# A two-layer attention trunk on one core: a sign flip moved behind a norm on ScalarE, two weight splits moved behind gate products on VectorE

## The chip, the cores and the metric

The kernel runs on one core of a Trainium2 chip. The metric is device microseconds of one execution. Three runs of the kernel before gave 819.14, 820.42 and 816.18 us, median 819.14 us. The execution that was profiled took 817.46 us.

The engines are called by the names that the profile uses: PE is TensorE's matmul, PEld its weight load, DVE is VectorE, ACT is ScalarE, POOL is GpSimd, SP is the queue that issues most of the loads.

## The reference, cut to what matters

Two decoder layers over 256 tokens of width 2048, then a final RMSNorm, all in float32.

```python
def rmsnorm(x, g):
    y = x * lax.rsqrt(jnp.mean(x * x, axis=-1, keepdims=True) + RMS_EPS)
    return y * g
# layer 0: forgetting attention, 32 heads of 64; logits += c[t] - c[s]
# layer 1: sliding window of 128, 32 query heads, 4 key heads, learned sinks:
m = jnp.maximum(jnp.max(s, axis=-1, keepdims=True), sink)
e = jnp.exp(s - m)
denom = jnp.sum(e, axis=-1, keepdims=True) + jnp.exp(sink - m)
o = jnp.einsum('bnhgqk,bnkhd->bnqhgd', e / denom, vw)
# both layers
y = y * jax.nn.silu(gate)
x = x + y @ w_out
```

The sinks are one learned number per head; they take part in the maximum and in the denominator of the second layer's softmax. Each layer's input projection yields queries, keys, values and a gate.

## The kernel before, in words

**Weights.** Every weight matrix is streamed from HBM once, in pieces of 128 x 1024 floats (512 KB). A piece lands in one of four raw buffers (`wraw`, issued from SP). `load` then splits it into a rounded high part, a cast on ScalarE (L222), and the exact remainder, the low part, a subtraction on VectorE (L223); the two stand in one of five buffers `w`. A raw buffer is free again when its low part is made. TensorE multiplies the high part with the activations' high and low halves in one wide product (512 columns) and the low part with the activations' high half in a narrow one (256 columns). In most units two pieces go together: the wide products of the first, the wide products of the second, then the narrow products of the first and of the second. So a piece's high part is needed some microseconds before its low part.

**Units and groups.** A unit is 256 output columns: four pieces, accumulated over 16 tiles of the inner dimension into a PSUM tile `acc` (two of them). Each unit ends in a function that reads `acc`. In the second layer a group `SwaGroup` has a query unit (`q`: rotation at L839 to L889, then the split `stack_q`, L366 and L367) and a gate unit (`gate_consumer`, L324, L325, and `silu`, L312 to L319). A group has two pairs of heads. A pair's scores go to the PSUM tile of the tag `S`, of which there is one (`ps_s2`, L453 to L460); L462 and L389 on VectorE add the mask and take the extreme, L337 and L902 on ScalarE are the exponentials, L353 and L356 normalise, L475 on VectorE transposes into `turned`. For every two groups `values` multiplies the probabilities with the values. For groups 1, 3 and 5 two of the four blocks of this product lie in the tag `S` tile (`psy_s`) and two in `psy` tiles; `some` multiplies them with the gates (the gate products, L962 for the first two blocks, L966 for the others) and then splits the result for the output projection (`spread`, L518 and L519). The next scores `ps_s2` can only be written when L962 has read `psy_s`, because both use the one tile.

**Order.** TensorE's instructions stay in the order in which the program issues them. Work of the attention is put between the matmuls by a count of steps: `after(n, fn)` calls `fn` n steps later. On the other engines a list scheduler orders the instructions, by its own estimates and by priorities (`tc.high_priority`); each engine then executes its list in that order.

**The sinks.** They are loaded by a DMA on POOL's queue during the first layer (L633, from the bias of the pair with head 8). L741, written in the second layer's `norm` right after its 1/rms, multiplies them by -1 on ScalarE into `sinks[:, 1, :]`; the score reductions of the second layer (L389) read this copy. The scheduler is free to place L741.

Of the kernel before, what the change touches and what calls it, by code (L numbers as in the profile page):

```python
# [10 lines left out]
F32 = mybir.dt.float32  # L11
F32R = mybir.dt.float32r
AF = mybir.ActivationFunctionType
ALU = mybir.AluOpType
# [45 lines left out]
def trunk(  # L60
# [16 lines left out]
    nc = tc.nc  # L77


    def mm(*args, **kw):  # L80
        tc.keep_in_program_order(nc.tensor.matmul(*args, **kw))  # L81
# [25 lines left out]
    def after(steps, fn):  # L107
        due.setdefault(clock[0] + max(steps, 1), []).append(fn)
# [23 lines left out]
    def inv_rms(sums, name, ps):  # L132
        for i, a in enumerate(sums):
            mm(ps[:, 0:S], ones, a, start=i == 0, stop=i == len(sums) - 1)
        v = cpool.tile([P, S], F32, tag="rms_v", name=f"v_{name}")
        nc.vector.tensor_scalar(v, ps[:, 0:S], 1.0 / D, EPS, op0=ALU.mult, op1=ALU.add)
        both = cpool.tile([P, S + 2], F32, tag="rms_r", name=f"r_{name}", bufs=2)
        r = both[:, 0:S]
        nc.scalar.activation(r, v, AF.Ln)
        nc.scalar.activation(r, r, AF.Exp, scale=-0.5)  # L140

        t = cpool.tile([P, S], F32, tag="rms_t", name=f"t_{name}")
        nc.vector.scalar_tensor_tensor(out=t, in0=r, scalar=-0.5, in1=r, op0=ALU.mult, op1=ALU.mult)
        nc.vector.tensor_mul(t, t, v)
        nc.vector.scalar_tensor_tensor(out=r, in0=t, scalar=1.5, in1=r, op0=ALU.add, op1=ALU.mult)

        for th in range(2):
            nc.vector.tensor_tensor_reduce(
                out=t[:, 0:P], in0=r[:, th * P : (th + 1) * P], in1=ident, scale=1.0, scalar=0.0,
                op0=ALU.mult, op1=ALU.add, accum_out=both[:, S + th : S + th + 1],  # L150
            )
        return both

    def split_x(kt, layer):
        g = g_sb[:, layer, kt : kt + 1]
        nc.scalar.activation(xs[:, kt, 0, :], xT[:, kt, :], AF.Copy, scale=g)  # L156
        nc.vector.scalar_tensor_tensor(
            out=xs[:, kt, 1, :], in0=xT[:, kt, :], scalar=g, in1=xs[:, kt, 0, :].bitcast(F32),
            op0=ALU.mult, op1=ALU.subtract,
        )  # L160
# [25 lines left out]
    state = {}  # L186
    asked = set()

    def ask(unit, p, eng):
        src, off, total, _, _ = unit.parts[p]  # L190
        n = unit.n
        if off == 0 and (unit, p) not in asked:
            asked.add((unit, p))
            given = unit.stages[p] if p < len(unit.stages) else None
            if given is None:
                raw = wpool.tile([P, 1024], F32, tag="wraw", name="wraw", bufs=4)
            else:
                pool, tag, size, bufs = given
                raw = pool.tile([P, size], F32, tag=tag, name="wraw", bufs=bufs)
            raw = raw[:, 0 : total * n]  # L200
            if isinstance(src, tuple):

                raw = raw.rearrange("p (g k n) -> p g k n", g=2, k=total)
                for g in range(2):
                    eng.dma_start(out=raw[:, g], in_=src[g])
                raw = raw.rearrange("p g k n -> p k g n")
            else:
                raw = raw.rearrange("p (k n) -> p k n", n=n)
                eng.dma_start(out=raw, in_=src)
            unit.raw = raw  # L210

    def load(unit, p):
        src, off, _, _, s = unit.parts[p]
        n = unit.n
        ask(unit, p, nc.sync)
        raw = unit.raw[:, off : off + s, :]
        w = wpool.tile([P, 2048], F32R, tag="w", name="w")
        w = w[:, 0 : 2 * s * n].rearrange("p (k h n) -> p k h n", h=2, n=n)
        high, low = w[:, :, 0, :], w[:, :, 1, :]
        if isinstance(src, tuple):  # L220
            high, low = (a.rearrange("p k (g n) -> p k g n", g=2) for a in (high, low))
        state["split"] = nc.scalar.copy(high, raw)  # L222
        nc.vector.tensor_tensor(out=low, in0=raw, in1=high.bitcast(F32), op=ALU.subtract)  # L223
        loaded[unit, p] = w

    def block(unit, p, c):
        _, _, _, kt0, s = unit.parts[p]
# [77 lines left out]
    def whole(src, kind, consume, **kw):  # L305
        return Unit(quarters(src), kind, consume, **kw)
# [221 lines left out]
    ones_row, z, a = (once[0:H, i * S : (i + 1) * S] for i in range(3))  # L528
# [182 lines left out]
    def square_into(sums, m):  # L711
        s = work.tile([P, 2, S], F32, tag="half", name="sq", bufs=HALVES)[:, 0, :]
        nc.scalar.activation(s, xT[:, m, :], AF.Square)  # L713
        if m == 0:
            acc = cpool.tile([P, S], F32, tag="ssq", name="acc", bufs=2)
            sums.append(acc)
            nc.gpsimd.tensor_copy(acc, s)  # L717
        else:
            nc.gpsimd.tensor_add(sums[0], sums[0], s)  # L719
# [5 lines left out]
    def to_layer1(m):  # L725
        split_x(m, 1)
        square_into(sums1, m)
        if m == KT - 1:

            def norm():  # L730
                nonlocal swa
                fox_scope.__exit__(None, None, None)
                swa = ctx.enter_context(tc.tile_pool(name="swa", bufs=2))
                state["r1"] = r = inv_rms(
                    sums1, "n1", ps_s.tile([P, 2, 512], F32, tag="S", name="ps_n1")[:, 0, :]
                )
                rope = swa.tile([P, 2, S], F32, name="rope_c", bufs=1)
                nc.sync.dma_start(out=rope, in_=rope_d)
                nc.vector.tensor_mul(rope, rope, r[:, 0:S].unsqueeze(1).to_broadcast([P, 2, S]))
                state["rr"] = rope  # L740
                nc.scalar.mul(state["sinks"][:, 1, :], state["sink"], -1.0)  # L741
                after(20, tail_residual)

            after(19, norm)
# [135 lines left out]
    class SwaGroup(Group):  # L880
# [50 lines left out]
        def some(self, together, mine, pair=None):  # L931

            kv = self.u // 2
            turned, vr = self.other.pts, state["vr"]
            banks = {} if pair is None else {a: pair[:, a] for a in range(2)}
            for a in mine:
                if a not in banks:
                    banks[a] = ps_t.tile([P, 512], F32, tag="T", name="psy")
            wanted = {}
            for a in mine:  # L940
                by_block = [(0, list(range(a + 1))), (1, list(range(a, NB + a + 1)))]
                wanted[a] = [(qb, k, k == ks[0], k == ks[-1]) for qb, ks in by_block for k in ks]
            for i in range(max(map(len, wanted.values()))):
                for a in mine:
                    if i >= len(wanted[a]):
                        continue
                    qb, k, first, last = wanted[a][i]
                    rows = slice(a * B, (a + 1) * B)
                    for hh in range(2):
                        out = banks[a][hh * HD : (hh + 1) * HD, 0 : 8 * B]  # L950
                        out = out.rearrange("p (n b i) -> p n b i", n=4, b=2)[:, :, qb, :]
                        o = qb * P + k * B
                        mm(
                            out, vr[k][rows, kv * HD : (kv + 1) * HD], turned[rows, :, hh, o : o + B],
                            start=first, stop=last, skip_group_check=True, tile_position=(a * B, hh * HD),
                        )
            for g, G in enumerate(together):
                y = G.gt.rearrange("p j (b a i) -> p a (j b) i", b=2, a=NB)
                here = slice(g * 4 * B, (g + 1) * 4 * B)
                if pair is not None:  # L960
                    both = pair[:, :, here].rearrange("p a (m i) -> p a m i", i=B)
                    nc.vector.tensor_mul(y[:, 0:2], both, y[:, 0:2])  # L962
                for a in mine:
                    if pair is None or a >= 2:
                        one = banks[a][:, here].rearrange("p (m i) -> p m i", i=B)
                        nc.vector.tensor_mul(y[:, a], one, y[:, a])  # L966
                if NB - 1 in mine:
                    self.spread(G)

    swa_units = [whole(swa_in_d[8], "wgt", swa_k), whole(swa_in_d[9], "tok", swa_v)]  # L970
    swa_groups = [SwaGroup(u) for u in range(8)]
# [64 lines left out]
    def fetch(upto):  # L1036
        while fetched[0] < min(upto, len(stream)):
            load(*stream[fetched[0]])
            fetched[0] += 1
# [127 lines left out]
```

## Time and profile before

| | |
|---|---|
| three runs | 816.18, 819.14, 820.42 us |
| profiled execution | 817.46 us |
| its span, first to last instruction | 815.7 us |
| busy share: PE, PEld, DVE, ACT, POOL | 99%, 87%, 77%, 65%, 8% |
| DMA, mean over the span | 186 GB/s |
| mean granted clock of TensorE | 0.998 |
| chain that ended last, by engine | PE 84%, DVE 8%, ACT 3%, DMA 3%, issue 1% |

The span leaves out 1.76 us of the execution's own time. A row of the timeline reads: start in us, duration in us, engine, line, operation, what is written from what, shapes, count, and in brackets how long the engine stood idle before it and what ended that. A row of the waits reads: who waited for whom, total us, times, longest.

### The profile page before, as it was taken

What the parts mean: (1) busy time and instruction counts of PE and PEld (TensorE: products, weight loads), DVE (VectorE), ACT (ScalarE), POOL (GpSimd) and SP (SyncE); (2) the same over time, 40 slices, a digit from 0 to 9 for tenths busy, and PEclk for the clock granted to TensorE, in tenths of its full rate; (3) what the DMA queues carried; (4) which work ended last, traced back from release to release, by engine and by line L of the source; (5) the groups of instructions that cost most, each with busy time, mean ns of one, the idle gap of its engine ahead of it and who ended that gap; (6) DMA issues with size and microseconds to landing.
All of it is one profiled execution on the core that took longest, in us unless ns stands there. A gap on an engine that the chain in (4) does not pass through costs nothing.

```text
span 815.7 us, 13805 instructions
## 1 busy us (share of the span) xinstructions
PE 804.4 (99%) x5090; PEld 705.6 (87%) x5090; DVE 628.5 (77%) x1132; ACT 526.6 (65%) x979; POOL 65.5 (8%) x102
## 2 busy tenths in 40 slices
PE   9999999999999999999999999999999999999996
PEld 8988878888888888888888888888888888888886
DVE  6988765888568875788848667669989889896645
ACT  6775665665657665576747455567788777875552
POOL 1013020010000100000002110200000000001210
PEclk9999999999999999999999999999999999999999
DMA  9766556565664666565465655765545465465632
GB/s 292 256 205 230 187 178 200 181 205 170 200 190 153 213 198 191 169 211 186 156 187 173 196 183 197 201 181 184 173 136 185 151 205 171 134 210 170 204 130 104
DMA packets 47730, 151.84 MB, mean 186 GB/s; under 512 B 5696, under 2 KB 7648, under 8 KB 47664
## 3 DMA queue, kind: packets, MB, share of 16 engines
q1 hardware_dynamic: 44640, 141.84, 54.0%
q0 software_dynamic: 1872, 7.67, 3.4%
q10 hardware_dynamic: 1152, 1.47, 0.5%
q8 instruction: 40, 0.66, 0.3%
q14 instruction: 26, 0.21, 0.1%
HBM read 148.55 MB, written 2.41 MB: 185 GB/s over the span
## 4 chain that ended last, share of the span: by engine, by line
PE 84%; DVE 8%; ACT 3%; DMA 3%; issue 1%; DVEq 0%; SPq 0%; ACTq 0%
PE acc L81 78%; DVE w L223 3%; DMA wraw<-in_swa_in_dram 2%; PE ps_s L81 2%; PE psy L81 2%; PE pt L84 1%; ACT st L337 1%; DVE turned L475 1%; DVE st L389 1%; ACT st L356 1%; ACT w L222 0%; DMA wraw<-in_vf_dram 0%; DVE q L367 0%; DVE st L462 0%; ACT gate_e L312 0%
## 5 line engine op out<-in xcount | busy, mean ns | idle before, releaser
L81 PE MATMUL acc<-xs,w 128*128 128x512 f32 (+1 forms) x2624 | 474.8, 339 | 0.0
L81 PEld LDWEIGHTS acc<-xs,w 128*128 128x128 f32 x2624 | 404.7, 190 | 52.8 <-issue 0.7
L223 DVE TENSOR_TENSOR w<-wraw,w 128x1024 fp32r<-128x1024 f32 (+4 forms) x277 | 322.4, 1180 | 107.5 <-ACT w L222 106.7
L222 ACT CAST w<-wraw 128x1024 fp32r<-128x1024 f32 (+4 forms) x277 | 274.5, 1008 | 136.6 <-PE acc L81 89.8
L81 PE MATMUL acc<-ys,w 128*128 128x512 f32 (+1 forms) x960 | 169.4, 337 | 0.0
L81 PEld LDWEIGHTS acc<-ys,w 128*128 128x128 f32 x960 | 147.7, 189 | 20.4 <-issue 0.5
L81 PE MATMUL acc<-w,xs 128*128 128x512 f32 (+2 forms) x512 | 111.1, 364 | 0.5 <-ACT w L222 0.5
L81 PEld LDWEIGHTS acc<-w,xs 128*128 128x128 f32 x512 | 86.8, 191 | 14.3 <-ACT w L222 0.8
L337 ACT ACTIVATE st<-st,mx 128x128 f32<-128x128 f32 (+1 forms) x128 | 56.6, 444 | 12.7 <-DVE mx L640 11.6
L295 ACT COPY half<-acc 128x512 f32<-128x512 f32 x56 | 32.5, 581 | 9.1 <-PE acc L81 8.5
L81 PE MATMUL ps_s<-kk,q 128*128 128x256 f32 (+1 forms) x160 | 30.8, 306 | 0.2 <-DVE gt L962 0.2
L719 POOL TENSOR_TENSOR acc<-acc,sq 128x256 f32<-128x256 f32 x28 | 23.7, 848 | 89.0 <-ACT sq L713 87.9
L81 PEld LDWEIGHTS ps_s<-kk,q 128*128 128x128 f32 x160 | 24.6, 189 | 3.9 <-issue 1.2
L125 POOL TENSOR_SCALAR_AFFINE_SELECT bc<-bc 128x256 f32<-128x256 f32 x32 | 22.1, 708 | 71.4 <-DMA bc<-negc_d 71.4
L627 POOL DMA_DIRECT2D bc<-negc_d x16 | 8.9, 554 | 214.3 <-DVE st L420 152.3
L312 ACT ACTIVATE gate_e<-gt 128x512 f32<-128x512 f32 x16 | 10.1, 632 | 24.6 <-DVE gt L325 24.6
L429 ACT COPY pts<-pt 128x384 f32<-128x384 f32 x32 | 15.2, 476 | 14.9 <-PE pt L84 14.9
L475 DVE STREAM_TRANSPOSE turned<-st 128x768 f32<-128x768 f32 x16 | 15.6, 977 | 11.5 <-ACT st L356 11.5
L717 POOL COPY acc<-sq 128x256 f32<-128x256 f32 x2 | 1.3, 672 | 286.3 <-ACT sq L713 286.3
L337 ACT ACTIVATION_READ_ACCUMULATOR st<-st,mx 128x1 f32 x128 | 24.0, 188 | 0.0
L356 ACT ACTIVATE st<-st,rl 128x128 f32<-128x128 f32 x64 | 23.9, 445 | 0.0
L156 ACT ACTIVATE xs<-xT,g_sb 128x256 fp32r<-128x256 f32 x32 | 15.5, 501 | 12.8 <-DVE xT L699 12.0
(144 smaller groups left out, 591.1 us busy)
## 6 DMA issues: line engine op xcount, KB each, us to landing
wraw<-in_fox_in_dram SPq DMA_DIRECT2D x96, 512.0 KB, 4.5
wraw<-in_swa_in_dram SPq DMA_DIRECT2D x72, 512.0 KB, 4.4
wraw<-in_fox_out_dram SPq DMA_DIRECT2D x32, 512.0 KB, 4.0
wraw<-in_swa_out_dram SPq DMA_DIRECT2D x32, 512.0 KB, 4.3
wraw<-in_fox_in_dram SPq DMA_DIRECT2D x54, 256.0 KB, 4.4
bc<-negc_d POOLq DMA_DIRECT2D x16, 384.0 KB, 5.2
wraw<-in_vf_dram SPq DMA_DIRECT2D x4, 288.0 KB, 4.8
xT<-in_xt_dram SPq DMA_DIRECT2D x2, 512.0 KB, 7.8
```

What stands on the lines that cost most here:

```text
L81: tc.keep_in_program_order(nc.tensor.matmul(*args, **kw))
L125: return nc.gpsimd.affine_select(out=ap, in_=ap, compare_op=ALU.is_ge, fill=NEG, base=base, pattern=pattern, channel_multiplier=mult,)
L156: nc.scalar.activation(xs[:, kt, 0, :], xT[:, kt, :], AF.Copy, scale=g)
L222: state["split"] = nc.scalar.copy(high, raw)
L223: nc.vector.tensor_tensor(out=low, in0=raw, in1=high.bitcast(F32), op=ALU.subtract)
L295: nc.scalar.copy(s, ps[:, :, S : 2 * S])
L312: nc.scalar.activation(e, z, AF.Abs)
L337: nc.scalar.activation(st[:, hh, rng], st[:, hh, rng], AF.Exp, scale=sign, bias=nm[:, qb, hh : hh + 1], accum_out=l[:, qb, hh : hh + 1],)
L356: nc.scalar.mul(st[:, hh, rng], st[:, hh, rng], rl[:, qb, hh : hh + 1])
L429: nc.scalar.copy(group.new_pts(self.j, hh)[:, hh, self.j, :], pt[:, 0 : 3 * P])
L475: nc.vector.transpose(turned.rearrange("p h k -> p (h k)"), self.st.rearrange("p h k -> p (h k)"))
L719: nc.gpsimd.tensor_add(sums[0], sums[0], s)
```

## The change

Three edits. The multiplication by -1 of the sinks (L741, in the changed kernel L752) is told to keep its place in the program, which is behind the two activations that make 1/rms of the second layer. `load` remembers the last two low parts. And after the gate products of groups 1, 3 and 5, `ahead_of_lows` adds an ordering edge, without a semaphore, from the last gate product to each of these two: they come later on VectorE than the products.

```diff
@@ load
         state["split"] = nc.scalar.copy(high, raw)
-        nc.vector.tensor_tensor(out=low, in0=raw, in1=high.bitcast(F32), op=ALU.subtract)
+        state["lows"] = [*state.get("lows", [])[-1:], nc.vector.tensor_tensor(
+            out=low, in0=raw, in1=high.bitcast(F32), op=ALU.subtract
+        )]
         loaded[unit, p] = w
+
+    def ahead_of_lows(ins):
+
+        for low in state["lows"]:
+            tc.add_manual_dep(
+                low.ins, ins.ins.name,
+                mybir.DependencyInfo(mybir.DependencyClass.NoSync, mybir.DependencyReason.DATA),
+                reason="ahead_of_lows",
+            )
@@ norm, in to_layer1
                 state["rr"] = rope
-                nc.scalar.mul(state["sinks"][:, 1, :], state["sink"], -1.0)
+                tc.keep_in_program_order(nc.scalar.mul(state["sinks"][:, 1, :], state["sink"], -1.0))
                 after(20, tail_residual)
@@ SwaGroup.some
-                        nc.vector.tensor_mul(y[:, a], one, y[:, a])
+                        last = nc.vector.tensor_mul(y[:, a], one, y[:, a])
                 if NB - 1 in mine:
                     self.spread(G)
+            if pair is not None:
+                ahead_of_lows(last)
```

The instructions are the same ones. On PE, POOL and SP their order is the same too; on ACT and DVE it differs as follows. (Lines from 224 on stand 11 higher in the changed kernel, from the end of `some` on 13.)

On ACT in the first layer, where the changed sign stood: `pts` are copies of transposed probabilities, `vg` are values, `w` are casts of weights, `st` are exponentials. Before:

```order
L222 CAST w_1183<-wraw_1181 128x4x256
L429 COPY pts_1193<-pt_1189 128x384
L741 ACTIVATE sinks_302<-sinks_302 128x32
L429 COPY pts_1193<-pt_1211 128x384
L600 ACTIVATE vg_1220<-acc_953,r_n0_492 128x512 x2
L222 CAST w_1225<-wraw_1223 128x4x256
L222 CAST w_1265<-wraw_1263 128x4x256
L337 ACTIVATE st_1195,l_1242<-st_1195,mx_1196 128x128
```

The changed kernel has these rows there without the third one. It stands instead on ACT behind 1/rms of the second layer (`r_n1`), ahead of a cast:

```order
L139 ACTIVATE r_n1_4958<-v_n1_4956 128x256
L140 ACTIVATE r_n1_4958<-r_n1_4958 128x256
L752 ACTIVATE sinks_302<-sinks_302 128x32
L222 CAST w_4991<-wraw_4989 128x4x256
L306 COPY half_5004<-acc_4901 128x512
```

On DVE at the gate products of group 1 (groups 3 and 5 have the same rows with other numbers): `q2` is the split of a query unit, `w` low parts, `gt` the gate products, `ys` their split, `st` the scores. Before:

```order
L367 TENSOR_TENSOR q2_5738<-rot_t_5729,q2_5738 64x2x256 x2
L223 TENSOR_TENSOR w_5776<-wraw_5774,w_5776 128x4x256
L223 TENSOR_TENSOR w_5789<-wraw_5787,w_5789 128x4x256
L962 TENSOR_TENSOR gt_5317<-psy_s_5815,gt_5317 128x2x4x32
L962 TENSOR_TENSOR gt_5574<-psy_s_5815,gt_5574 128x2x4x32
L966 TENSOR_TENSOR gt_5317<-psy_5816,gt_5317 128x4x32
L966 TENSOR_TENSOR gt_5574<-psy_5816,gt_5574 128x4x32
L966 TENSOR_TENSOR gt_5317<-psy_5817,gt_5317 128x4x32
L966 TENSOR_TENSOR gt_5574<-psy_5817,gt_5574 128x4x32
L223 TENSOR_TENSOR w_5892<-wraw_5890,w_5892 128x4x256
L519 TENSOR_TENSOR ys_81<-gt_5317,ys_81 128x2x256
L519 TENSOR_TENSOR ys_81<-gt_5574,ys_81 128x2x256
```

Now:

```order
L378 TENSOR_TENSOR q2_5738<-rot_t_5729,q2_5738 64x2x256 x2
L973 TENSOR_TENSOR gt_5317<-psy_s_5815,gt_5317 128x2x4x32
L973 TENSOR_TENSOR gt_5574<-psy_s_5815,gt_5574 128x2x4x32
L977 TENSOR_TENSOR gt_5317<-psy_5816,gt_5317 128x4x32
L977 TENSOR_TENSOR gt_5574<-psy_5816,gt_5574 128x4x32
L977 TENSOR_TENSOR gt_5317<-psy_5817,gt_5317 128x4x32
L977 TENSOR_TENSOR gt_5574<-psy_5817,gt_5574 128x4x32
L223 TENSOR_TENSOR w_5776<-wraw_5774,w_5776 128x4x256
L223 TENSOR_TENSOR w_5789<-wraw_5787,w_5789 128x4x256
L530 TENSOR_TENSOR ys_81<-gt_5317,ys_81 128x2x256
L530 TENSOR_TENSOR ys_81<-gt_5574,ys_81 128x2x256
L473 TENSOR_TENSOR st_5929<-ps_s2_5931,smask_291 128x2x128
```

The two low parts went behind all six products, and the low part `w_5892` behind the first step of the scores. The scheduler then also orders what follows in another way, up to the next query unit's split. On DVE at that unit's rotation (`rot`), before:

```order
L319 TENSOR_TENSOR gt_5903<-gt_5903,gate_e_5908 128x512
L841 STREAM_SHUFFLE rot_6062<-rot_t_6058 128x512
L223 TENSOR_TENSOR w_6047<-wraw_6045,w_6047 128x4x256
L844 TENSOR_TENSOR rot_t_6058<-rot_t_6058,rope_c_4967 128x512
L845 TENSOR_TENSOR rot_6062<-rot_6062,rope_c_4967 128x512
L475 STREAM_TRANSPOSE turned_6080<-st_6002 128x768
L889 TENSOR_TENSOR rot_t_6058<-rot_t_6058,rot_6062 128x512
L223 TENSOR_TENSOR w_6074<-wraw_6072,w_6074 128x4x256
L367 TENSOR_TENSOR q2_6067<-rot_t_6058,q2_6067 64x2x256 x2
```

Now:

```order
L852 STREAM_SHUFFLE rot_6062<-rot_t_6058 128x512
L486 STREAM_TRANSPOSE turned_6080<-st_6002 128x768
L855 TENSOR_TENSOR rot_t_6058<-rot_t_6058,rope_c_4967 128x512
L856 TENSOR_TENSOR rot_6062<-rot_6062,rope_c_4967 128x512
L330 TENSOR_TENSOR gt_5903<-gt_5903,gate_e_5908 128x512
L900 TENSOR_TENSOR rot_t_6058<-rot_t_6058,rot_6062 128x512
L223 TENSOR_TENSOR w_6047<-wraw_6045,w_6047 128x4x256
L223 TENSOR_TENSOR w_6074<-wraw_6072,w_6074 128x4x256
L378 TENSOR_TENSOR q2_6067<-rot_t_6058,q2_6067 64x2x256 x2
```

The low part `w_6047` went behind the rotation. The low parts `w_5976` and `w_5989`, which stood behind the second pair's extremes (L389), now stand ahead of them, and on ACT their casts stand ahead of the first pair's normalising (L356, now L367) instead of behind it, while the gate's activations (L312 and on) stand behind it.

## The prediction

> **What bounds the kernel now.** First the shares of the page, then the waits of TensorE's two queues, since a change on ScalarE and VectorE can only bring what TensorE waits for them.
>
> ```profile
> span 815.7 us, 13805 instructions
> PE 804.4 (99%) x5090; PEld 705.6 (87%) x5090; DVE 628.5 (77%) x1132; ACT 526.6 (65%) x979; POOL 65.5 (8%) x102
> ...
> PE rows L81 <- DVE tail L800: 2.1, 1, 2.1
> PE pt L84 <- DVE st L348: 1.8, 1, 1.8
> ...
> PE ps_s L81 <- DVE gt L962: 0.2, 1, 0.2
> ...
> PEld pt L84 <- ACT st L337: 2.0, 1, 2.0
> ...
> PEld ps_s L81 <- issue: 1.2, 3, 0.6
> ```
>
> TensorE bounds it: 804.4 of 815.7 us are matmul. Besides the start and the tail there are two kinds of hole. One is a single wait of 1.8 us (matmul row) or 2.0 us (weight-load row) of transposes `pt` for normalised probabilities. The other is small and stands ahead of three score products `ps_s`: 0.2 us by the matmul row, 1.2 us in three by the weight-load row. The change is aimed at these two, so 2.0 to 3.2 us is all it can take away.
>
> **The sign of the sinks.** The timeline around the one big hole:
>
> ```profile
> 104.16 0.47 ACT L429 COPY pts<-pt 128x384 f32<-128x384 f32 x1
> ...
> 105.62 0.49 PE L84 MATMUL pt<-ident,st 128*128 128x128 f32 x3
> ...
> 105.87 1.17 PE L81 MATMUL acc<-w,xs 128*128 128x512 f32 x4
> ...
> 109.35 0.08 DVE L389 DVE_READ_ACCUMULATOR2_ANT mx<- 128x1 f32 x1
> ...
> 110.43 0.23 ACT L741 ACTIVATE sinks<-sinks 128x32 f32<-128x32 f32 x1 [5.80 <-DMA sinks<-in_sink_dram]
> ...
> 110.93 1.27 ACT L600 ACTIVATE vg<-acc,r_n 128x512 f32<-128x512 f32 x2
> 112.08 2.00 ACT L222 CAST w<-wraw 128x1024 fp32r<-128x1024 f32 x2
> ...
> 113.17 1.26 DVE L223 TENSOR_TENSOR w<-wraw,w 128x1024 fp32r<-128x1024 f32 x1 [3.73 <-ACT w L222]
> ...
> 114.94 0.41 ACT L337 ACTIVATE st<-st,mx 128x128 f32<-128x128 f32 x1 [0.86 <-DVE mx L640]
> ...
> 117.49 0.61 PE L84 MATMUL pt<-ident,st 128*128 128x128 f32 x3 [1.81 <-DVE st L348]
> ```
>
> ScalarE stands 5.80 us at the sign flip, until the sinks' DMA lands at 110.43. Queued behind it are a copy of `pts`, the values `vg`, two casts, and the exponentials of the next pair; VectorE's low part waits 3.73 us for the first of those casts, with the pair's extremes (L639, L640) behind it, and TensorE waits for the pair.
>
> Without the flip: the second `pts` copy can start when its transposes end (105.62 + 0.49 = 106.11) and takes 0.47, to 106.58. The values need the last `acc` products (105.87 + 1.17 = 107.04), so they run from 107.04 to 108.31. The casts follow without a wait in the old rows, to 110.31, the first one done at about 109.3. VectorE is free at 109.43, so its low part starts there instead of at 113.17. From its start to the exponentials took 114.94 - 113.17 = 1.77, which gives 111.20, and from there to the transposes on TensorE 117.49 - 114.94 = 2.55, which gives 113.75. TensorE itself only arrives at about 117.49 - 1.98 = 115.5. So the inputs are 1.75 us early, and the whole hole closes: **-2.0 us** (the weight-load row; -1.8 by the matmul row). If a cast had to wait for a landing or a buffer that the stall now hides, up to 1.75 us of that costs nothing.
>
> At its new place the flip has company:
>
> ```profile
> 501.18 0.42 ACT L140 ACTIVATE r_n<-r_n 128x256 f32<-128x256 f32 x1
> ...
> 502.41 1.05 ACT L222 CAST w<-wraw 128x1024 fp32r<-128x1024 f32 x1 [0.81 <-PE acc L81]
> ```
>
> Its 0.23 us fall into the 0.81 us in which the next cast waits for TensorE anyway, and its DMA landed some 390 us earlier: **0**. If that cover were gone, it would delay one cast by 0.23 us.
>
> **The two low parts.** The three places, seen on TensorE and VectorE (first and second place, and the third's weight load):
>
> ```profile
> 585.63 3.29 PE L81 MATMUL acc<-xs,w 128*128 128x256 f32 x18
> 585.66 2.36 DVE L223 TENSOR_TENSOR w<-wraw,w 128x1024 fp32r<-128x1024 f32 x2
> ...
> 587.94 0.75 DVE L962 TENSOR_TENSOR gt<-psy_s,gt 128x256 f32<-128x256 f32 x2
> 588.60 0.88 DVE L966 TENSOR_TENSOR gt<-psy,gt 128x128 f32<-128x128 f32 x4
> 588.80 0.77 PEld L81 LDWEIGHTS ps_s<-kk,q 128*128 128x128 f32 x6 [0.30 <-issue]
> 588.83 0.95 PE L81 MATMUL ps_s<-kk,q 128*128 128x256 f32 x6
> ...
> 635.68 3.29 PE L81 MATMUL acc<-xs,w 128*128 128x256 f32 x18
> ...
> 639.14 0.95 PE L81 MATMUL ps_s<-kk,q 128*128 128x256 f32 x6 [0.16 <-DVE gt L962]
> ...
> 689.25 0.77 PEld L81 LDWEIGHTS ps_s<-kk,q 128*128 128x128 f32 x6 [0.39 <-issue]
> ```
>
> The values' products have ended when `acc` resumes at 585.63, but the gate products only start at 587.94, behind 2.36 us of low parts. They free the one score tile at 588.69, and `ps_s` starts right then, at 588.83. With the products ahead they run from about 585.7 to 586.4 for the score tile, over 2 us before TensorE asks for it. These holes close too.
>
> Their size: the 18 matmuls ahead are 10 narrow and 8 wide. The pace of each comes from two pieces of the chain of waits, wide and then narrow:
>
> ```profile
> 88.17 2.32 PE acc L81 x10
> ...
> 164.51 1.18 PE acc L81 x10
> ```
>
> That is 0.232 and 0.118 us, so 18 need 10 x 0.118 + 8 x 0.232 = 3.04 us. They took 588.83 - 585.63 = 3.20 and 639.14 - 635.68 = 3.46: 0.16 and 0.42 lost; the third, whose weight-load gap of 0.39 lies between the first's 0.30 and the second's 1.2 - 0.30 - 0.39 = 0.5, about 0.25. Together 0.83, of which I leave some for the resumption after the values' products, which stays. Bounds 0.2 (matmul wait) and 1.2 (weight-load gaps); I take **-0.6 us**, nearer to the spacing of the matmuls than to either.
>
> [...]
>
> What the two low parts lose: `w_5776` ends some 1.5 us later (the six products, 587.94 to 589.48), near 588.4. Its narrow products come behind six scores, eight wide and eight narrow ones, 588.83 + 0.79 + 1.86 + 0.94 = 592.4. Free by 4 us; `w_5789` has more. **0**.
>
> **What moved further down.** The tightest is `w_6047`, now behind the rotation:
>
> ```profile
> 598.17 0.98 DVE L475 STREAM_TRANSPOSE turned<-st 128x768 f32<-128x768 f32 x1 [1.62 <-ACT st L356]
> ...
> 605.57 1.22 DVE L223 TENSOR_TENSOR w<-wraw,w 128x1024 fp32r<-128x1024 f32 x1
> 606.69 0.69 DVE L844 TENSOR_TENSOR rot_t<-rot_t,rope_c 128x512 f32<-128x512 f32 x1
> ...
> 609.36 1.23 DVE L223 TENSOR_TENSOR w<-wraw,w 128x1024 fp32r<-128x1024 f32 x1
> ...
> 612.65 0.88 PE L81 MATMUL ps_s<-kk,q 128*128 128x256 f32 x6
> ```
>
> The rows from 606.69 to 609.36 (2.67 us) go ahead of it, so it ends at 606.79 + 2.67 = 609.46 if VectorE keeps its pace. TensorE wants it ahead of eight narrow and eight wide matmuls that precede the scores at 612.65: 612.65 - 0.94 - 1.86 = 609.85, about 0.1 earlier once the first hole is gone. That leaves 0.3 us, where there were 3. What widens it: VectorE's wait of 1.62 us at 598.17 is now filled, as `w_5976` and `w_5989` stand there. I price it at **0**; between a gain of nothing and a loss of 1 us in each of three places (VectorE over a microsecond behind its old pace).
>
> **Sum.** -2.0 - 0.6 = -2.6 us. On the profiled execution: 817.46 - 2.6 = 814.9, of which 1.76 lie outside the span, which would be 813.1. The median shown lies 1.7 above that execution and would give 816.5. The four executions have a mean of 818.3, and I take that level: **815.7 us**.
>
> **The rivals.**
>
> *A: the new order waits for a landing (slower).* On ScalarE the casts of `w_5976` and `w_5989` now stand ahead of the first pair's normalising. The raw buffer of `w_5976` is the one that `w_5776` frees, so its load starts at 588.4 instead of 586.9.
>
> ```profile
> wraw<-in_swa_in_dram SPq DMA_DIRECT2D x72, 512.0 KB, 4.4
> ...
> 527.50 10.62 DMA wraw<-in_swa_in_dram
> ```
>
> With the usual 4.4 us it lands at 592.8; the cast's turn comes near 595, so nothing waits. With the 10.62 of the chain's longest it lands at 599.0, 4 us late; normalising, transposition and rotation, and with them `w_6047`, come 4 us late, of which the filled wait absorbs 1 at most: 3 us in each of three places, 9 - 2.6 = 6.4 slower, 824.7 us. It decides from landings over 7 us. For it: such a landing exists in this layer. Against: it stands where the values' own round trip loads the DMA. 5%.
>
> *B: VectorE runs short after all.* The 0.3 us at `w_6047` are overdrawn by 1 us a place: +3 - 2.6 = 0.4 slower, 818.7 us. For: VectorE shows next to no idle there but the 1.62. Against: just that wait is now filled. 9%.
>
> *C: the big hole is handed on.* The transposes wait for something that the flip hid (the landing of the casts' pieces), and only the small holes close: -0.6, 817.7 us. For: both casts ran in the shadow of the flip, so the rows don't show when their data came. Against: 1.75 us of margin. 8%.
>
> *D: the small holes don't close* (the scores wait for the query split instead): -2.0, 816.3 us. Against: that split is over when the low parts start at 585.66, 3 us ahead of the scores. 10%.
>
> The forecast has the remaining 68%.
>
> **How the numbers follow.** The three runs shown spread over 4.2 us, so two medians of three can differ by some 1.7 us by chance alone, and half a percent, 4.1 us, is about what can be told from no change. Faster by over 0.5% needs 1.5 us of such chance on top of -2.6, about one time in five: 0.68 x 0.2, with D's 0.1 x 0.12 and a little from the others, 0.16. Slower by over 0.5% is A and a sliver of B: 0.05. The rest, 0.79, is within. No case gains over 3.2 us by itself. The range for 8 in 10 goes from 812 (the bound of -3.2 and the chance spread downwards) to 819.5, which holds B, C and D; A is left out.
>
> **What would show it.** Right: ScalarE's wait of 5.80 us for the sinks' DMA is gone, the row of `pt` waiting for L348 near 115 us is gone, the gate products (now L973) start right behind the query split, and the three scores behind them show no weight-load gap; busy times of all engines stay as they are. Wrong: a wait of TensorE's narrow products for VectorE's low parts after each of the three places (B), a cast waiting for a landing ahead of L367 (A), or a new wait of `pt` for L222's followers (C). If the time fell by more than 4 us with only these holes closed, the reading of TensorE's idle time was too narrow.

## The result, and the profile after

The changed kernel took 814.67 us (median of 6 executions, 813.63 to 814.94), the kernel before, on the same chip, 818.80 us (median of 6, 816.18 to 820.42). The ratio is 0.995, with a 95% interval of 0.9933 to 0.9967: faster by half a percent, 4.1 us. The predicted time was 815.7 us. The range, 812 to 819.5 us, also holds the kernel before (818.80 us), so that the time fell in it says little of the mechanism; the change and the traces say more. The execution that was profiled took 814.94 us, where the sum had 814.9; but 4.1 us are more than the 2.6 us of that sum, and the times lie within 1.3 us of one another where those of the kernel before spread over 4.2 us. The experiments are about these two surprises.

First the page of the changed kernel: its span, the busy times by engine, and what TensorE's matmuls waited for.

```profile
span 813.2 us, 13799 instructions
PE 803.5 (99%) x5090; PEld 705.6 (87%) x5090; DVE 629.2 (77%) x1132; ACT 527.1 (65%) x979; POOL 62.5 (8%) x102
```

```profile
PE rows L81 <- DVE tail L811: 2.1, 1, 2.1
PE warm L81 <- DVE ones L118: 1.1, 1, 1.1
PE acc L81 <- ACT w L222: 0.8, 2, 0.5
```

The rows of `pt` and of `ps_s` are gone, and nothing new stands beside the tail and the start. The span is 2.5 us shorter; the busy times are within 1 us of what they were, but for POOL's, 3.0 us less. The timeline of the changed kernel where the big hole stood (ScalarE and TensorE), at the flip's new place, and at the first gate products:

```profile
106.46 0.48 ACT L440 COPY pts<-pt 128x384 f32<-128x384 f32 x1 [1.52 <-PE pt L84]
...
107.39 1.27 ACT L611 ACTIVATE vg<-acc,r_n 128x512 f32<-128x512 f32 x2 [0.45 <-PE acc L81]
...
111.41 0.39 ACT L348 ACTIVATE st<-st,mx 128x128 f32<-128x128 f32 x1
...
115.83 0.49 PE L84 MATMUL pt<-ident,st 128*128 128x128 f32 x3
...
499.74 0.21 ACT L752 ACTIVATE sinks<-sinks 128x32 f32<-128x32 f32 x1
500.64 1.05 ACT L222 CAST w<-wraw 128x1024 fp32r<-128x1024 f32 x1 [0.69 <-PE acc L81]
...
583.47 0.76 DVE L973 TENSOR_TENSOR gt<-psy_s,gt 128x256 f32<-128x256 f32 x2 [1.58 <-PE psy_s L81]
583.87 3.30 PE L81 MATMUL acc<-xs,w 128*128 128x256 f32 x18
...
584.94 2.35 DVE L223 TENSOR_TENSOR w<-wraw,w 128x1024 fp32r<-128x1024 f32 x2
587.00 0.88 PE L81 MATMUL ps_s<-kk,q 128*128 128x256 f32 x6
```

ScalarE goes on at 106.46 when the transposes end, and TensorE meets its next transposes at 115.83 without a wait. This execution started 0.31 us later (its first loads came later), so the predicted positions hold to a tenth: `vg` at 107.04 + 0.31 = 107.35, the exponentials at 111.20 + 0.31 = 111.51, TensorE at 115.5 + 0.31 = 115.8. The flip costs nothing at its new place: the cast behind it still waits 0.69 us for TensorE. The gate products come first behind the query split, wait 1.58 us for the values' products, and start 3.5 us ahead of the scores that need their tile (583.47 against 587.00), where they started 0.89 us ahead of them before.

With the 5090 matmuls of the two traces set side by side, the start of the changed kernel's falls behind by 0.31 us in the first loads, gains 2.05 at `pt`, and then 0.16, 0.39 and 0.23 at the three places of `ps_s`: +0.31 - 2.05 - 0.78 = -2.5, the difference of the spans. So the two traces agree with the prediction. The two medians do not: 1.6 us more went somewhere.

### The profile page after: what moved, and what is told of

The parts are those of the page before. It is cut to its first block, busy times and chain, and to the rows that moved or that the text cites. A ratio compares the mean times of both kernels' runs of the same rounds, so it can differ in the third digit from the quotient of the medians.

```text
span 813.2 us, 13799 instructions
## 1 busy us (share of the span) xinstructions
PE 803.5 (99%) x5090; PEld 705.6 (87%) x5090; DVE 629.2 (77%) x1132; ACT 527.1 (65%) x979; POOL 62.5 (8%) x102
## 4 chain that ended last, share of the span: by engine, by line
PE 98%; DMA 1%; DVE 0%; ACT 0%; SPq 0%; DVEq 0%; issue 0%
PE acc L81 91%; PE ps_s L81 3%; PE psy L81 2%; PE pt L84 1%; DMA wraw<-in_fox_in_dram 1%; PE psy_s L81 0%; DVE scaled L825 0%; PE ps_n L81 0%; DVEq L1174 0%; PE rows L81 0%; DVE tail_x L797 0%; PE pt_r L84 0%; DVE rest L801 0%; SPq L209 0%; ACT w L222 0%
## 5 line engine op out<-in xcount | busy, mean ns | idle before, releaser
L125 POOL TENSOR_SCALAR_AFFINE_SELECT bc<-bc 128x256 f32<-128x256 f32 x32 | 19.0, 614 | 71.5 <-DMA bc<-negc_d 71.5
L367 ACT ACTIVATE st<-st,rl 128x128 f32<-128x128 f32 x64 | 23.9, 445 | 0.1
L157 DVE SCALAR_TENSOR_TENSOR xs<-xT,g_sb,xs 128x256 fp32r<-128x256 f32 x32 | 16.8, 544 | 6.7 <-ACT xs L156 6.7
```

The source lines that it names most:

```text
L125: return nc.gpsimd.affine_select(out=ap, in_=ap, compare_op=ALU.is_ge, fill=NEG, base=base, pattern=pattern, channel_multiplier=mult,)
L157: nc.vector.scalar_tensor_tensor(out=xs[:, kt, 1, :], in0=xT[:, kt, :], scalar=g, in1=xs[:, kt, 0, :].bitcast(F32), op0=ALU.mult, op1=ALU. ...
L367: nc.scalar.mul(st[:, hh, rng], st[:, hh, rng], rl[:, qb, hh : hh + 1])
```

## The parts one by one

Four kernels ran on one chip beside 20 executions of the kernel before (median 818.32 us, 814.94 to 819.74).

**The whole change again.** No edit.

> The changed kernel again, beside its parts on one chip. The sum of the prediction gives 2.6 us less than the kernel before; the first comparison of medians gave about 4.1 us, its profile's span 2.5 us. Theory H1: the landing of the sinks' load comes earlier or later from execution to execution, so that the hole of the kernel before is 1.8 us in the execution that was profiled and up to some 5 us in others; then the changed kernel is again 3 to 4.5 us shorter than the kernel before, and its times lie within 1.5 us of one another, those of the kernel before within 3 to 5 us. Theory H2: the difference beyond 2.6 us was chance; then the medians lie 2 to 3.2 us apart this time, and both kernels spread alike.

Measured: 814.36 us (814.04 to 814.99), ratio 0.9953 (0.9937 to 0.9969). 4.0 us again: not chance. The spread is 0.95 us against 4.8.

**The flip alone.**

```diff
-                nc.scalar.mul(state["sinks"][:, 1, :], state["sink"], -1.0)
+                tc.keep_in_program_order(nc.scalar.mul(state["sinks"][:, 1, :], state["sink"], -1.0))
```

> The kernel before, with the sign flip of the sinks alone moved behind the second layer's 1/rms. By the sum: -2.0 us (-1.8 to -2.1), profiled span near 813.7 us; the wait of 5.80 us on ScalarE is gone, the one of the transposes of about 1.8 us on TensorE too, while the three small holes ahead of the scores stay. H1 (the hole varies with the landing): the median lies 2.5 to 3.8 us below that of the kernel before, that is within 1 us of the whole change, and the times of this kernel lie within 1.5 us of one another. H2 (chance): about 2 us below, with the spread of the kernel before.

Measured: 814.83 us (814.15 to 815.49), ratio 0.9956 (0.994 to 0.9971), span 812.5 us. This part alone gives 3.5 of the 4.0 us and the whole narrowing. TensorE's waits in its trace:

```profile
PE rows L81 <- DVE tail L800: 2.1, 1, 2.1
PE acc L81 <- ACT w L222: 1.1, 2, 0.6
PE warm L81 <- DVE ones L118: 1.1, 1, 1.1
```

One expectation failed: I had the small holes ahead of the scores stay, and there is no row of `ps_s` here, although the low parts stand in their old place.

**The two low parts alone.** The edit is the change without its line on the sinks.

> The kernel before, with the two low parts alone put behind the gate products; the flip stays where it was. By the sum: -0.6 us (the difference of the two traces of before and after, matmul by matmul, gives -0.8 for the three places together), profiled span near 815.0 us; ScalarE still waits some 5 to 6 us for the sinks' load, and TensorE's transposes some 1.8 us behind it. H1: the median lies 0.4 to 1.2 us below that of the kernel before, and the times spread over 3 us or more, as the kernel before does; the wait for the sinks in this profile may differ from 5.80 us by a microsecond or more. H2: 0.6 to 0.8 us below, the wait within 0.3 us of 5.80.

Measured: 818.29 us (814.61 to 819.61), ratio 1.0002 (0.9986 to 1.0017). The low parts by themselves bring nothing that shows in the median; I had expected 0.4 us or more. The spread of 5 us stays, as does the wait for the sinks, 5.60 us, and the hole of 1.74 us behind it:

```profile
110.52 0.23 ACT L752 ACTIVATE sinks<-sinks 128x32 f32<-128x32 f32 x1 [5.60 <-DMA sinks<-in_sink_dram]
...
117.70 0.61 PE L84 MATMUL pt<-ident,st 128*128 128x128 f32 x3 [1.74 <-DVE st L359]
```

**The place kept, the load earlier.**

```diff
-SINK = 8
+SINK = 2
-                nc.scalar.mul(state["sinks"][:, 1, :], state["sink"], -1.0)
+                flip = nc.scalar.mul(state["sinks"][:, 1, :], state["sink"], -1.0)
+                tc.add_manual_dep(flip.ins, state["copies"][4].ins.name, ...)  # its old place
```

> The kernel before, with the flip kept at its old place in ScalarE's row, and only the load of the sinks issued some 25 us earlier, ahead of three more loads on GpSimd's queue. Theory of the prediction: the flip costs only by waiting for the landing, so with the load long there it costs its own 0.23 us on ScalarE, hidden in front of TensorE; the result is that of moving the flip: -2.0 us by the sum, -2.5 to -3.8 with H1, times within 1.5 us of one another. Rival: it is the place in the row (the order on ScalarE) and not the landing that makes the hole; then the time stays at that of the kernel before, 0 +- 0.5 us, and transposes still wait about 1.8 us. A second rival, price from the profile: the earlier load delays a masked softmax load behind it on GpSimd's queue by its 0.55 us; up to +0.55 us if that is on TensorE's path.

Measured: 815.20 us (814.14 to 816.42), ratio 0.9963 (0.9947 to 0.9978). The load is issued at 65.9 us instead of 106 (40 us earlier, not 25), and the flip, still between the two copies of `pts`, waits for nothing:

```profile
104.30 0.23 ACT L743 ACTIVATE sinks<-sinks 128x32 f32<-128x32 f32 x1
```

So it was the landing and not the place in ScalarE's row, and 3.1 of the 4 us come from it. The rival that the place decides falls. One expectation failed: the times spread over 2.3 us and not 1.5. The trace has the small holes, some 0.9 us in all.

## Three more traces of the kernel before

What one trace of the kernel before cannot show is how its executions differ. Of the 61 on record, the three of this section among them, 10 took 814.3 to 816.0 us, 12 took 816.1 to 818.0, and 39 took 818.0 to 820.8. So three more were traced, with no edit. (These were the last runs; those of the next two sections came before them.)

> The kernel before, unchanged, once more, for the trace of another execution: its times fall into groups (of 50 executions nine took 814.3 to 816, the others 817 to 820.8), and one trace holds one of them. H3 with the landing (the theory by now): what differs is the wait of ScalarE for the sinks' load, and behind it the hole of TensorE, and whether the granted clock falls to a half behind the hole for some 3.4 us. An execution of 818 to 820 us then shows a hole of 2 us or more and a stretch of half clock between 118 and 123 us, one of 814.3 to 816 shows a hole of less than a microsecond and a full clock, one near 817.3 a hole of 1.7 to 2 us and a full clock. Rival: the groups come from another place (the small holes, the start), and hole and clock at 118 us are those of the first trace whatever the time.

> As the run before it: the kernel before once more, for one more trace. By the theory its time, less 815.7 + 1.76 us of the first trace, equals the growth of the hole of the transposes beyond 1.8 us, plus half of the stretch of half clock behind it, to within 0.8 us. By the rival, these stay at 1.8 and 0 whatever the time.

> As the two runs before it: a third trace of the kernel before, with the same expectations. Three executions should hold at least one with the half clock (some 24 of 30 executions were above 817.7 us).

They took 814.57, 818.62 and 816.19 us: one of each kind. The issue of the sinks' load with the step ahead of it on GpSimd, the flip and the transposes in the timeline of the first, which took 814.57 us, and behind them its first gate products:

```profile
102.88 0.81 POOL L125 TENSOR_SCALAR_AFFINE_SELECT bc<-bc 128x256 f32<-128x256 f32 x2 [3.81 <-DMA bc<-negc_d]
...
103.64 0.55 POOL L633 DMA_DIRECT2D sinks<-in_sink_dram  x1
...
106.89 0.23 ACT L741 ACTIVATE sinks<-sinks 128x32 f32<-128x32 f32 x1 [2.30 <-DMA sinks<-in_sink_dram]
...
115.47 0.49 PE L84 MATMUL pt<-ident,st 128*128 128x128 f32 x3
...
581.73 2.36 DVE L223 TENSOR_TENSOR w<-wraw,w 128x1024 fp32r<-128x1024 f32 x2
584.01 0.75 DVE L962 TENSOR_TENSOR gt<-psy_s,gt 128x256 f32<-128x256 f32 x2
...
586.65 0.88 PE L81 MATMUL ps_s<-kk,q 128*128 128x256 f32 x6
```

The same in the second, 818.62 us, with four windows behind it (the column ahead of the last two is the granted clock: the share of its full clock that TensorE was given):

```profile
102.68 3.11 POOL L125 TENSOR_SCALAR_AFFINE_SELECT bc<-bc 128x256 f32<-128x256 f32 x2 [3.97 <-DMA bc<-negc_d]
...
105.75 0.55 POOL L633 DMA_DIRECT2D sinks<-in_sink_dram  x1
...
110.69 0.23 ACT L741 ACTIVATE sinks<-sinks 128x32 f32<-128x32 f32 x1 [6.46 <-DMA sinks<-in_sink_dram]
...
117.86 0.70 PE L84 MATMUL pt<-ident,st 128*128 128x128 f32 x3 [2.58 <-DVE st L348]
118.23 2.89 PE L81 MATMUL acc<-xs,w 128*128 128x512 f32 x8
```

```profile
116.00:118.00 2.00, 0.14 (x1) 0.14 (x1) 1.17 (x5) 2.00 (x7) 0.00 (x0) 1.00 0.81 264
118.00:120.00 2.00, 2.00 (x7) 1.66 (x7) 2.00 (x4) 1.44 (x3) 0.00 (x0) 0.56 0.61 223
120.00:122.00 2.00, 2.00 (x10) 1.89 (x9) 0.93 (x2) 0.79 (x2) 0.00 (x0) 0.58 0.63 213
122.00:124.00 2.00, 2.00 (x11) 1.63 (x10) 1.90 (x3) 1.97 (x4) 0.00 (x0) 1.00 0.69 217
```

And in the third, 816.19 us:

```profile
109.70 0.23 ACT L741 ACTIVATE sinks<-sinks 128x32 f32<-128x32 f32 x1 [5.57 <-DMA sinks<-in_sink_dram]
...
116.88 0.61 PE L84 MATMUL pt<-ident,st 128*128 128x128 f32 x3 [1.70 <-DVE st L348]
```

Three things are to be seen.

The wait for the sinks is a different one each time: 2.30, 5.57 and 6.46 us, where the first trace had 5.80. TensorE's hole behind it is the wait less some 3.9 us: none, 1.70, 2.58 (and 1.81). The load is issued at 103.6 us in the first of the three and at 105.7 in the others, and it lands 3.2, 4.9 and 4.0 us later; in all the traces of this study that issue it there, the landing takes 3.2 to 5.3 us. So it is not the landing alone that varies: of the 3.8 us between the landings in the first of the three and in the second, 2.1 are the issue. The masks of L125 ahead of it on GpSimd took 0.81 us in the first and 3.11 in the second; all ten other traces issue it at 105.5 to 106.5 us. Why the masks were shorter this once is open.

In the second, the granted clock of TensorE falls behind the hole, to a mean of 0.56 and 0.58 in two windows. They lack 0.44 x 2 and 0.42 x 2 = 1.72 us of full clock, which at one half (0.50, as whole windows of two traces below show) is a stretch of 3.4 us. The same eight matmuls take 2.89 us instead of 1.64, and by the end of the stretch the matmuls have fallen back a further 1.58 us. The hole costs its own length and then 1.6 us more. In the third, and in the first trace of all, a hole of 1.7 to 1.8 us left the clock at 1.00.

The small holes come and go as well. The first of these traces is 2.89 us shorter than the profiled execution of the prediction: 2.08 at `pt`, and 0.8 at the three places of `ps_s`, with the low parts in their old order. There VectorE began the two low parts at 581.73, before the values' products ended (`acc` resumes at 583.51), and the gate products behind them stood 2.6 us ahead of the scores; in the trace of the prediction it began them at 585.66, just as `acc` resumed. Why VectorE is nearly 2 us later in one execution than in another stays open.

For these three traces the rival, that the groups come from elsewhere than hole and clock, falls: hole and clock change with the time. For the other executions only the mean granted clock is on record. Of 35 above 818 us, 25 have 0.994 or 0.995, which none of 46 executions of kernels without the big hole has (0.996 to 0.998); the other ten have 0.996 or 0.998, so whether each of them lost clock is not shown. My rule for the times doesn't hold to the 0.8 us that I gave it, though: growth of the hole and half of the stretch give -1.8, +2.5 and -0.1 us against the profiled execution, and measured were -2.9, +1.2 and -1.3. It leaves out the small holes, up to 0.8 us, and the first loads, up to 0.5. With them the second is start -0.40, hole +0.77, clock +1.58, small holes -0.78, together +1.17 against 818.62 - 817.46 = 1.16.

## The load made later

```diff
                     with tc.issue_after(filled.ins):
+                        spare = fox.tile([P, 3, 32], F32, name="spare", bufs=1)
+                        for i in range(3):
+                            nc.gpsimd.dma_start(out=spare[:, i], in_=sink_d.partition_broadcast(P))
                         nc.gpsimd.dma_start(out=state["sink"], in_=sink_d.partition_broadcast(P))
```

(The flip is kept at its old place in ScalarE's row, as with the earlier load.)

> The kernel before, with three more loads like the sinks' one (into a tile that nothing reads) issued right ahead of it, so that it is issued and lands some 1.65 us (3 x 0.55) later and the hole of TensorE grows from 1.8-2.0 to about 3.5 us; the order of every other instruction is that of the kernel before. The last runs brought a third theory: of 20 executions of the kernel before, those with a mean granted clock of 0.994 or 0.995 took 818.1 to 819.7 us, those with 0.997 took 815.3 to 817.7, while every execution without the hole had 0.996 to 0.998. H3 (the clock): the hole makes the throttle grant TensorE less for a stretch behind it, in some executions and not in others, and 0.0025 x 816 = 2 us are lost on top of the hole itself. Then with a hole of 3.5 us this happens in every execution or nearly: a median near 817.2 + 1.65 + 2 = 820.9 us, all clocks 0.993 to 0.995, and in the profile the granted clock is below 1.00 in the microseconds behind 119 us. H1 (only the landing varies, and the hole with it): 818.3 + 1.65 = 820.0 us, the granted clock stays at 1.00 behind the hole.

Measured: 823.13 us (820.70 to 825.14), ratio 1.0065 (1.0047 to 1.0084), beside a kernel before at 818.38 us (30 executions). The load was issued at 108.3 us and landed 6.8 us later, later than I had reckoned, so the hole was 5.64 us and not 3.5. The transposes and the windows in its trace:

```profile
121.88 0.88 PE L84 MATMUL pt<-ident,st 128*128 128x128 f32 x3 [5.64 <-DVE st L348]
```

```profile
118.00:120.00 2.00, 0.00 (x0) 0.00 (x0) 1.97 (x4) 1.38 (x4) 0.00 (x0) 0.99 0.00 0
120.00:122.00 2.00, 0.12 (x1) 0.15 (x1) 1.18 (x5) 2.00 (x7) 0.00 (x0) 0.50 0.79 236
122.00:124.00 2.00, 2.00 (x7) 1.69 (x8) 2.00 (x4) 1.46 (x3) 0.00 (x0) 0.50 0.73 246
124.00:126.00 2.00, 2.00 (x10) 1.90 (x9) 0.75 (x2) 0.59 (x2) 0.00 (x0) 0.50 0.69 213
126.00:128.00 2.00, 2.00 (x8) 1.59 (x8) 1.90 (x3) 2.00 (x3) 0.00 (x0) 0.81 0.66 213
```

The clock falls to a half at about 120 us, while TensorE still stands, and comes back near 126.8: 6.8 us, twice the 3.4 of the trace above. Matmul by matmul, the hole grew by 3.83 us against the first trace, and 2.20 more went in the half clock behind it. Eight of the nine executions had a mean granted clock of 0.992 to 0.994, the ninth 0.996. So the longest of the holes, 5.64 us, brought the most lost clock, 3.40 us of full clock against 1.72 behind that of 2.58, and with the clock at 1.00 at this place in every trace without a hole, the theory that only the landing varies falls: here the clock went with the landing. My number for the median (820.9) was 2.2 us short, because of the later landing and the doubled stretch.

## VectorE's margin at the three places

Additions of 128x256 with unused results were put ahead of the gate products at each of the three places, each 0.42 us, three of them about 1.3 us.

```diff
+            late = state["q_split"]
+            for _ in range(3 if pair is not None else 0):
+                one = nc.vector.tensor_add(idle, *[ones.unsqueeze(1).to_broadcast([P, 2, P])] * 2)
+                behind(one, late)
+                late = one
...
-                    nc.vector.tensor_mul(y[:, 0:2], both, y[:, 0:2])
+                    behind(nc.vector.tensor_mul(y[:, 0:2], both, y[:, 0:2]), late)
```

**Three of them in the kernel before.**

> The kernel before, with three additions of 128x256 on VectorE (about 0.4 us each, results unused) between the two low parts ahead of the gate products, at each of the three places where the change moves the low parts; nothing else moves. Theory of the prediction: the small holes ahead of the scores are VectorE's lateness with the gate products, which is already more than nothing, so each of the three holes grows by the whole 1.1 to 1.2 us: +3.4 us (3.0 to 3.7), span near 819.1 us; TensorE's row of the scores waiting for the gate products rises from 0.2 to some 3 us or more. Rival: the weight-load gaps ahead of the scores have another cause (TensorE's own resumption), and VectorE has margin there: below +1.5 us.

Measured: 821.13 us, ratio 1.0037 (1.002 to 1.0053), that is +3.0 us (1.6 to 4.3) against the kernel before; by the medians it is +2.75. Its profiled execution has a span of 818.5 us, 2.8 above the first trace. In this trace the first place shows no hole at all; the second and the third lose 0.24 and 0.97 us more than they did there. 1.8 of the 2.8 us are at the big hole, which is 0.24 us longer here (2.04) and brings the half clock with it, 1.58. But the first trace is a poor one to compare with, for it has small holes and no half clock. Against the trace of 818.62 us, which has the half clock and no small holes, this one is 1.7 us longer (820.32), and the second and the third place lose 0.6 and 1.2 us. The waits, and two windows:

```profile
PE pt L84 <- DVE st L348: 2.0, 1, 2.0
PE ps_s L81 <- DVE gt L976: 1.4, 2, 1.0
```

```profile
118.00:120.00 2.00, 2.00 (x10) 1.72 (x10) 2.00 (x4) 1.30 (x2) 0.00 (x0) 0.67 0.54 184
120.00:122.00 2.00, 2.00 (x9) 1.81 (x9) 1.36 (x3) 1.39 (x3) 0.00 (x0) 0.50 0.73 229
```

So theory and rival are each right for a part: the dose does open holes at the places, but VectorE has margin there in some executions (the gate products stood 0.89 us ahead of the scores in the first trace and 2.64 in that of 814.57 us, 1.75 apart), and where it has margin, less than the whole dose is lost.

**Three in the changed kernel, and six.** The same edit, with 6 in place of 3 in the second.

> The changed kernel with the same three additions (about 1.1 us) ahead of the gate products at each of the three places, now ahead of the low parts too. From the trace of the changed kernel the scores find their tile free some 2.8 us early and the narrow products their low part 1.66 us early. Theory: 0 (+-0.5 us) against the changed kernel, no new wait of TensorE at the three places. Rival: VectorE's order now has no slack (my estimate for the low part was 0.3 us, not 1.66): 0.8 us a place, +2.4 us.

> The changed kernel with six such additions (about 2.3 us) at each of the three places. Theory: the scores still come in time (2.8 us of margin), the low part that now stands behind the rotation does not (1.66 us): 0.6 to 0.8 us a place, some +2 us (1 to 3) against the changed kernel, as a wait of TensorE's narrow acc products for VectorE's low part; this is the mechanism and place of the prediction's rival B. Rival: VectorE catches up in idle time between, 0.

Measured: three cost 0.8 us (815.12 us, ratio to the kernel before 0.9967, 0.9948 to 0.9986; the changed kernel had 0.9953), six cost 4.4 us (818.77 us, ratio 1.0011, 0.9993 to 1.0029), both by the medians against the changed kernel's 814.36. That run was on another chip; by the ratios to the kernel before they cost 1.1 and 4.7 us. The interval for three overlaps that of the changed kernel, so three can't be told from nothing; six lie above theory and rival. Two expectations failed: with three there are new gaps of TensorE, and with six the scores don't come in time. With six, TensorE waits for the gate products and, elsewhere in the layer, for casts and for extremes. The low part behind the rotation, which was to bring all of it, shows only as gaps of the weight loads of 0.2 us, at two places with three additions and at all three with six. Here are the waits of the matmuls with six, and the first of these gaps:

```profile
PE ps_s L81 <- DVE gt L987: 1.1, 2, 0.8
PE acc L81 <- ACT w L222: 1.1, 4, 0.6
...
PE ps_s L81 <- DVE mx L400: 1.0, 2, 0.7
```

```profile
608.72 2.63 PEld L81 LDWEIGHTS acc<-xs,w 128*128 128x128 f32 x16 [0.21 <-DVE w L223]
```

The margins that I read from one trace (2.8 us ahead of the scores, 1.66 ahead of the narrow products) overstate what VectorE has: the changed kernel takes 1.3 us more at each place for 0.8 us in all three, and the second 1.3 us costs 3.6 in all three, nearly its full length.

## Why the prediction was right, and where it was not

**The big hole** was read right: why it was there, that all of it closes, and where each instruction then stands. -2.0 us was priced, and 2.05 measured between the two traces. What was mis-sized is this term for other executions. The 1.8 us were the hole of one execution of 817.46 us. In the traced one of the largest group, 818.62 us, it was 2.58, because the landing is later, and the half clock took 1.6 us more: 4.2 us, which the sum had at 2.0. That is where the 4.0 us went: the flip alone brings 3.5 by the medians.

**The small holes**: -0.6 priced, -0.78 measured between the two traces, which confirms the spacing of the matmuls as the row to price them by (the matmul waits gave 0.2, the weight-load gaps 1.2). But they were a state of that execution. Of seven traces with the low parts in the old order and without a dose, two have holes of 0.8 to 0.9 us in all, one has a trace of one and four have none; in all traces of the new order without a dose they are gone. By the medians this part is worth nothing when it is alone, and 0.5 us on top of the flip (814.36 against 814.83), which these runs can't tell from nothing (the intervals of the two ratios overlap nearly whole).

**The level** is the step that failed. I added the distance of the shown executions to the sum: "The four executions have a mean of 818.3, and I take that level". This took their distance from the profiled execution for something that the change leaves alone. It was the same hole, longer, with the clock behind it, and it went with the flip; the sum on the profiled execution, 814.9, would have been nearer than 815.7. The three times shown spread over 4.2 us, and I took that for chance of the measurement, so a gain of over half a percent got a chance of only 0.16, most of it from that; the measured gain is half a percent. The spread had a cause that could have been asked for: which wait in the trace hangs on something that need not come at the same time twice.

**The rivals.** A (a landing that the new order waits for) didn't happen: the casts at the three places wait for no load in the changed kernel's trace. B (VectorE short at `w_6047`) didn't happen either: that low part ends at 606.29 and its first narrow product starts at 607.95, 1.66 us where I estimated 0.3. By then this trace is 1.90 us ahead of the first, so the product came when I had it (609.85) and VectorE 1.3 us sooner than "if VectorE keeps its pace". The wait of B appears with the doses, but only as gaps of 0.2 us. C (the hole handed on) and D (the small holes wait for the query split) are refuted by the waits of the changed kernel, D also by its margin: the query split is over at 581.90, 5.1 us ahead of the scores.

**The bound** of 3.2 us, "all it can take away", was the bound of one trace. The closing sentence had it the right way round: if more than 4 us went with only these holes closed, "the reading of TensorE's idle time was too narrow". It was: lost clock is not idle time, and no row of waits shows it (the 1.58 us in the trace of 818.62 us stand in none).

## What to carry to other kernels

An instruction that waits for a load on an engine's ordered list costs TensorE what the load's issue and landing make of it in the usual execution (here a hole of none, 1.70, 1.81 and 2.58 us in four traces of one kernel), which one trace need not show: where the times of a kernel spread, look for such a wait first, and price its removal with the spread. A hole of TensorE can cost more than its length: behind those of 2.04 and 2.58 us another 1.6 us went in clock, behind that of 5.64 us 2.2. The windows behind it tell, the waits don't. And margins on an engine that is nearly always busy in a stage (VectorE 30.6 of 32 us from 583 to 615 us in the changed kernel's trace) should be measured with a dose, since one execution's margin is not the next one's (0.89 and 2.64 us in two traces of the kernel before).

## What the runs showed of the hardware

The granted clock fell to 0.50 for 3.4 us behind holes of 2.04 and 2.58 us, and for 6.8 us around one of 5.64 us; holes of 1.70, 1.74 and 1.81 us left it at 1.00. The stretches are worked out from the windows at one half: in the trace with the hole of 2.04 us they lack 1.70 us of full clock (0.67, 0.50 and 0.98 from 118 to 124 us), in that of 2.58 us 1.72, in that of 5.64 us 3.40. No trace has a hole between 1.81 and 2.04 us here, and whether the length of the hole alone decides, these six cases don't tell.

A small broadcast load on GpSimd's queue, 128x32, took 3.2 to 5.3 us to land at one and the same place of the program (eleven traces), and 6.8 us behind three more of its kind.
